# A two-layer diffusion step on eight cores: a generated order per engine, tiles without halo columns, the residual in DRAM, and softmax sums in column tiles

## The chip, the cores and the metric

The kernel runs on all eight cores of one Trainium2 chip, two dies of four cores. Each core computes the same program on its own share of the batch. The metric is the device time of the slowest core, in microseconds (us). Some executions fall in a slow state, in which one die is granted a lower TensorE clock (one of experiment 1: 0.84 against 0.93, and 3288.53 us); verdicts use fast runs alone. A *ratio* below is the mean time of one kernel's fast runs over that of the kernel before in the same rounds on the same chip, with a 95% interval, so it is not quite the ratio of the medians quoted beside it, which are over all executions, slow ones too.

## The reference, cut to what matters

Two layers. Layer 0 mixes tokens with a gated short convolution, layer 1 with grouped-query attention (eight query heads, two key/value heads of 128). After each comes a feed-forward block with a width-3 depthwise convolution. RMS norms stand before and after each sub-layer.

```python
def short_conv_mixer(u, w_in, conv_k, w_out):
    b_gate, c_gate, xp = jnp.split(u @ w_in, 3, axis=-1)
    return (b_gate * dwconv3(c_gate * xp, conv_k)) @ w_out
def conv_ffn(u, w_up, conv_k, w_down):
    h = dwconv3(u @ w_up, conv_k)          # (B, L, 2*D_FF)
    g, up = jnp.split(h, 2, axis=-1)
    return (jax.nn.silu(g) * up) @ w_down
def gated_residual(h, y, g, gate):
    return h + gate * rms_norm(y, g)
# per layer (shortened):
#   u = rms_norm(h, g) * (1 + scale) + shift;  h = gated_residual(h, mixer(u), ...)
#   u = rms_norm(h, g) * (1 + scale) + shift;  h = gated_residual(h, conv_ffn(u), ...)
```

A core holds 3072 tokens of 1024 features: one sample of 2048 tokens, cut into the units S0 and S1 of 1024, and four prompts of 256, the unit PU. S0 and S1 are neighbours in the convolutions. A sample's queries attend to 2560 keys (512 cached), a prompt's to its own 256.

## The kernel before

It is tuned by hand. The text order of the program is the order on each engine, and Python generators are woven by fixed ratios. The second half of an output projection's residual update is *deferred*: it is put, two feature blocks at a time, between pieces of the next stage. Both of its operations run on VectorE (DVE).

```python
                def pair(p):
                    for m in (2 * p, 2 * p + 1):
                        ... P.op("dve", lambda e, m=m: e.scalar_tensor_tensor(   # y = y * gate * rstd
                        ... P.op("dve", lambda e, m=m: e.tensor_tensor(          # h = h + y
                if ct == 0:
                    for p in range(4):
                        pair(p)
                else:
                    for p in range(4):
                        deferred_tail.append((p, lambda p=p: pair(p)))
```

The softmax sums are a 128-row matmul with a matrix of ones for every key chunk, as long as the value matmul beside it.

```python
                def pv(item, first, last):
                    ... e.matmul(bank(ob, NQ), vb[:, vch, j * 128:(j + 1) * 128], pt[pi][:, 0:NQ], ...
                    ... e.matmul(bank(db, NQ), ones, pt[pi][:, 0:NQ], start=first, stop=last)
                ...
                    if ki == min(1, len(keys) - 1) and pending_fin:
                        pending_fin.pop(0)()
```

The whole residual `h` stays in SBUF, the core's working memory. The convolution's inputs are computed with one or two extra halo columns per tile, the neighbours that the width-3 convolution needs (2688 small matmuls), in two sets of three banks of PSUM, the memory in which matmul results land.

Of the kernel before, what the change touches and what calls it, by code (L numbers as in the profile page):

```python
# [11 lines left out]
D = 1024  # L12
# [9 lines left out]
UW = 1032  # L22
# [11 lines left out]

class Prog:
    def __init__(self, nc, es):
        self.nc = nc
        self.engs = {"pe": nc.tensor, "act": nc.scalar, "dve": nc.vector, "pool": nc.gpsimd, "sp": nc.sync}
        self.sems = {}
        self.cnt = {}  # L40
        for e in self.engs:
            self.sems[e] = es.enter_context(nc.semaphore("s_" + e))
            self.cnt[e] = 0
        self.dsem = {}
        self.dcnt = {}
        self.dnext = {"pool": 0, "sp": 0}
        self.ND = 12
        for q in ("pool", "sp"):
            for i in range(self.ND):
                k = "d_%s%d" % (q, i)  # L50
                self.sems[k] = es.enter_context(nc.semaphore(k))
                self.cnt[k] = 0
        self.waited = {}
        self.lastw = {}
        self.readers = {}
        self.out_events = []

    def _need(self, reads, writes):
        need = {}

        def add(ev):
            if ev is None:
                return
            k, v = ev
            if need.get(k, 0) < v:
                need[k] = v
        for r in reads:
            add(self.lastw.get(r))
            if isinstance(r, tuple) and r[0] == "ps":
                for ev in self.readers.get(r, ()):  # L70
                    add(ev)
        for w in writes:
            add(self.lastw.get(w))
            for ev in self.readers.get(w, ()):
                add(ev)
        return need

    def _emit_waits(self, e, need):
        eng = self.engs[e]
        for k, v in need.items():  # L80
            if e == "pe" and k == "pe":
                continue
            if self.waited.get((e, k), 0) < v:
                eng.wait_ge(self.sems[k], v)
                self.waited[(e, k)] = v

    def _record(self, ev, reads, writes):
        for r in reads:
            self.readers.setdefault(r, []).append(ev)
        for w in writes:  # L90
            self.lastw[w] = ev
            self.readers[w] = []

    def op(self, e, fn, reads=(), writes=()):
        need = self._need(reads, writes)
        self._emit_waits(e, need)
        ins = fn(self.engs[e])
        self.cnt[e] += 1
        ins.then_inc(self.sems[e], 1)
        ev = (e, self.cnt[e])  # L100
        self.waited[(e, e)] = max(self.waited.get((e, e), 0), 0)
        self._record(ev, reads, writes)
        return ev

    def dma(self, q, out, in_, reads=(), writes=(), is_output=False):
        i = self.dnext[q]
        self.dnext[q] = (i + 1) % self.ND
        k = "d_%s%d" % (q, i)
        need = self._need(reads, writes)
        if self.cnt[k] > 0:  # L110
            need[k] = max(need.get(k, 0), self.cnt[k])
        self._emit_waits(q, need)
        self.engs[q].dma_start(out=out, in_=in_).then_inc(self.sems[k], 16)
        self.cnt[k] += 16
        ev = (k, self.cnt[k])
        self._record(ev, reads, writes)
        if is_output:
            self.out_events.append(ev)
        return ev

    def barrier(self, engs=("pe", "act", "dve")):
        for e in engs:
            need = {p: self.cnt[p] for p in engs if self.cnt[p] > 0}
            self._emit_waits(e, need)

    def finish(self):
        need = {}
        for k, v in self.out_events:
            need[k] = max(need.get(k, 0), v)
        self._emit_waits("sp", need)  # L130

def run(gen):
    for _ in gen:
        pass

def weave(main, side, per):
    main = iter(main)
    side = iter(side)
    credit = 0.0
    m_alive = True  # L140
    s_alive = True
    while m_alive:
        try:
            next(main)
        except StopIteration:
            m_alive = False
            break
        credit += 1.0
        while s_alive and credit >= per:
            credit -= per  # L150
            try:
                next(side)
            except StopIteration:
                s_alive = False
    if s_alive:
        for _ in side:
            pass

def build_program():
# [21 lines left out]
    rrot = din("rrot", [128, 128])  # L181
    h_out = dout("h_out", [128, KC, TT])
    k_out = dout("k_out", [128, 2, TP])
    v_out = dout("v_out", [TP, 256])

    with ExitStack() as es:
        P = Prog(nc, es)

        def sb(name, cols, dt):
            return es.enter_context(nc.sbuf_tensor(name, [128, cols], dt))  # L190

        h_t = sb("h", KC * TT, F32)
        ru_t = sb("ru", KC * UW, BF16)
        ry_t = sb("ry", KC * 516, F32)
        ra_t = sb("ra", NCF * 1024, BF16)
        wsl_t = [sb("wsl%d" % i, 3072, BF16) for i in range(3)]
        SQ = [sb("sq%d" % i, 512, BF16) for i in range(4)]
        FB = [sb("fb%d" % i, 512, F32) for i in range(4)]
        par_t = sb("par", P_N, F32)
        ones_t = sb("ones", 128, BF16)  # L200
        rrot_t = sb("rrotsb", 128, F32)
        silu_t = sb("silu", 16, BF16)
        modT_t = sb("modT", 2 * 96, F32)
        coef_t = sb("coef", 2 * 64, F32)
        hsave_t = sb("hsave", KC, F32)
        dummy_t = sb("dmy_scr", 2, F32)
        ps_t = es.enter_context(nc.psum_tensor("ps", [128, 4096], F32))

        h = h_t[:].rearrange("p (k t) -> p k t", k=KC)
        u = ru_t[:].rearrange("p (k t) -> p k t", k=KC)  # L210
        ybuf = ry_t[:].rearrange("p (k t) -> p k t", k=KC)
        evq = [ry_t[:, 516 * i:516 * i + 512] for i in range(8)]
        EVQK = [("RY", i) for i in range(8)]
        ev = [ry_t[:, i * 1032:(i + 1) * 1032] for i in range(4)]
        EVK = [[("RY", 2 * i), ("RY", 2 * i + 1)] for i in range(4)]
        pt = [ry_t[:, 516 * (4 + i):516 * (4 + i) + 256].bitcast(BF16) for i in range(4)]
        PTK = [("RY", 4 + i) for i in range(4)]
        a3 = ra_t[:].rearrange("p (c t) -> p c t", c=NCF)
        ps = ps_t[:]
        par = par_t[:]  # L220
        ones = ones_t[:]

        def bank(b, n=512, off=0):
            return ps[:, b * 512 + off: b * 512 + off + n]

        def switch_view():
            pass

        P.dma("sp", par, params, writes=["par"])
        def load_x(ui, after=()):  # L230
            for kc in range(KC):
                P.dma("sp", h[:, kc, ui * 1024:(ui + 1) * 1024], x_in[:, kc, ui * 1024:(ui + 1) * 1024],
                      reads=list(after), writes=[("h", kc, 2 * ui), ("h", kc, 2 * ui + 1)])
        load_x(0)
        P.dma("sp", rrot_t[:], rrot, writes=["rrot"])
        P.op("dve", lambda e: e.memset(ones, 1.0), writes=["ones"])
        P.op("act", lambda e: e.activation(out=silu_t[:], in_=par[:, P_CVEC:P_CVEC + 16], func=AF.Silu),
             reads=["par"], writes=["silu"])
        eps_ap = par[:, P_EPS:P_EPS + 1]

        wstate = {"i": 0}

        def load_w(src, ncols):
            i = wstate["i"]
            wstate["i"] = (i + 1) % 3
            P.dma("pool", wsl_t[i][:, 0:ncols], src, writes=[("w", i)])
            return i

        def wv3(i, inner, nk=KC):
            return wsl_t[i][:, 0:nk * inner].rearrange("p (k n) -> p k n", n=inner)  # L250
# [4 lines left out]
        def mod_gen(l, parts):  # L255
            mv, cf = mvs[l], cfs[l]
            g = lambda which: par[:, P_GAIN + l * 32 + which * 8: P_GAIN + l * 32 + which * 8 + 8]
            for part in parts:
                for bi in range(4):
                    blk = part * 4 + bi  # L260
                    si = load_w(modw[l, blk], KC * 256)
                    w3 = wv3(si, 256)
                    for j in range(2):
                        ch = blk * 2 + j

                        def f(e, w3=w3, j=j, ch=ch):
                            for kc in range(KC):
                                ins = e.matmul(bank(6, 2, ch * 2), w3[:, kc, j * 128:(j + 1) * 128],
                                               silu_t[:, kc * 2:kc * 2 + 2], start=(kc == 0), stop=(kc == KC - 1))
                            return ins  # L270
                        P.op("pe", f, reads=[("w", si), "silu"], writes=[("ps", 6)])
# [49 lines left out]
        def vcols(flat, U, shift):  # L321
            if U.sample:
                return flat[:, 1 + shift:1025 + shift]
# [643 lines left out]
```

## Time and profile before

The time before is 3163.78 us, the median of three runs (3155.91 to 3164.3).

| of the profiled core | before |
|---|---|
| TensorE (PE) busy, and idle | 2731.7, 435.8 us |
| of the busy time, lost to the clock at half speed or at 0.81 | 75 us |
| PE busy less that loss, the *floor* | 2657 us |
| DVE, ACT, POOL busy | 1763, 1484, 229 us |

The loss is worked out from the trace: busy time in each stretch of lower clock, times one minus that clock.

### The profile page before, as it was taken

To read this page: it belongs to the slowest core of one execution; us is meant where nothing else is said; L and a number is where in the kernel's file an instruction comes from. 1 tells how busy PE (TensorE), PEld (TensorE's weight loads), DVE (VectorE), ACT (ScalarE), POOL (GpSimd) and SP (SyncE) were. 2 spreads that over 40 slices of the span, in tenths; PEclk is the share of its full clock that TensorE was granted. 3 is DMA by queue.
4 is the path that set the end of the run, shared out by engine and by line. 5 is a ranking of instruction groups with operands and counts; after the bars stand their busy time and mean duration, and the time that the engine had idled before them with its cause. 6 is when DMAs were issued, how large, how long until landed. Compare 5 with 4: busy or idle time off the path is not lost.

```text
span 3167.5 us, 44493 instructions; the slowest of 8 cores (3146.7 to 3167.5 us)
## 1 busy us (share of the span) xinstructions
PE 2731.7 (86%) x15052; PEld 1245.2 (39%) x15052; DVE 1763.1 (56%) x2113; ACT 1484.0 (47%) x2387; POOL 229.0 (7%) x435
## 2 busy tenths in 40 slices
PE   1889897899899989996799979997779998998997
PEld 0434343344344444442234324443234444443443
DVE  2354555785577477545434363433368647846762
ACT  2142424444344433343588648875834434443432
POOL 0010101000001001000000100001000000000000
PEclk9999999999999999998999999999989999999999
DMA  8655454336555745652100310015234474365347
GB/s 190 114 90 99 71 97 67 64 68 107 93 107 107 127 87 94 108 106 54 30 1 1 54 27 1 1 16 96 35 59 73 84 132 98 67 119 127 67 82 151
DMA packets 72203, 251.16 MB, mean 79 GB/s; under 512 B 7984, under 2 KB 9520, under 8 KB 71984
## 3 DMA queue, kind: packets, MB, share of 16 engines
q0 software_dynamic: 62192, 217.61, 40.7%
q1 hardware_dynamic: 9792, 30.72, 2.9%
q8 instruction: 127, 2.08, 0.3%
q14 instruction: 92, 0.75, 0.1%
HBM read 451.19 MB, written 14.68 MB: 147 GB/s over the span
## 4 chain that ended last, share of the span: by engine, by line
PE 64%; DVE 14%; ACT 8%; DMA 7%; issue 6%; SPq 0%; DVEq 0%; ACTq 0%; POOLq 0%; POOL 0%
PE ps L478 29%; PE ps L421 16%; PE ps L743 5%; PE ps L745 4%; PE ps L753 4%; DVE ry L566 3%; DVE ry L569 3%; PE ps L608 2%; DVE ry L448 2%; DVE h L451 2%; DMA wsl<-wup 2%; DMA wsl<-wo 1%; DMA h<-x_in 1%; ACT ry L561 1%; DVE fb L384 1%
## 5 line engine op out<-in xcount | busy, mean ns | idle before, releaser
L478 PE MATMUL ps<-ru,wsl 128*128 128x512 bf16 (+2 forms) x8064 | 1298.0, 313 | 109.8 <-DVE ry L569 75.6
L478 PEld LDWEIGHTS ps<-ru,wsl 128*128 128x128 bf16 x8064 | 620.2, 98 | 787.5 <-issue 176.8
L421 PE MATMUL ps<-ra,wsl 128*128 128x512 bf16 x2880 | 666.2, 385 | 33.4 <-DMA wsl<-wo 12.6
L566 DVE SCALAR_TENSOR_TENSOR ry<-ps,par,ry 128x1024 f32<-128x1024 f32 x264 | 338.5, 1282 | 193.2 <-ACT ry L558 119.4
L421 PEld LDWEIGHTS ps<-ra,wsl 128*128 128x128 bf16 x2880 | 280.7, 99 | 379.0 <-issue 67.9
L755 ACT ACTIVATE ry<-ps 128x512 bf16<-128x512 f32 x672 | 387.7, 596 | 83.0 <-PE ps L753 41.1
L569 DVE SCALAR_TENSOR_TENSOR ry<-ps,par,ry 128x1024 f32<-128x1024 f32 x264 | 338.8, 1283 | 28.3 <-DVE ry L566 0.9
L384 DVE SCALAR_TENSOR_TENSOR fb<-h,coef,fb 128x512 f32<-128x512 f32 (+2 forms) x296 | 173.6, 587 | 233.7 <-ACT fb L336 233.5
L743 PE MATMUL ps<-ry,ra 128*128 128x512 bf16 x672 | 257.2, 383 | 42.3 <-ACT ry L755 27.0
L448 DVE SCALAR_TENSOR_TENSOR ry<-ry,coef,fb 128x512 f32<-128x512 f32 x192 | 143.2, 746 | 236.9 <-ACT fb L336 236.9
L770 DVE RECIPROCAL fb<-ps 128x512 f32<-128x512 f32 x32 | 107.4, 3358 | 275.8 <-PE ps L745 247.7
L745 PE MATMUL ps<-ry,ones 128*128 128x512 bf16 x672 | 257.3, 383 | 0.0
L435 ACT ACTIVATE ry<-ps 128x512 f32<-128x512 f32 x192 | 113.6, 591 | 299.8 <-PE ps L421 249.9
L753 PE MATMUL ps<-ra 128*128 128x512 bf16 x672 | 245.0, 382 | 7.5 <-DVE ry L640 4.7
L558 ACT ACTIVATE ry<-ps,par 128x513 f32<-128x513 f32 x176 | 121.2, 689 | 204.1 <-PE ps L478 202.8
L556 ACT ACTIVATE ry<-ps,par 128x511 f32<-128x511 f32 x176 | 120.9, 687 | 204.7 <-PE ps L478 126.2
L561 ACT ACTIVATE ry<-ps,par 128x1024 f32<-128x1024 f32 x88 | 98.1, 1114 | 244.2 <-PE ps L478 205.1
L361 ACT ACTIVATE sq<-h 128x512 bf16<-128x512 f32 (+2 forms) x296 | 136.8, 496 | 158.4 <-PE ps L366 126.3
L366 PE MATMUL ps<-sq,ones 128*128 128x512 bf16 (+2 forms) x320 | 93.0, 320 | 118.4 <-ACT sq L361 114.4
L573 DVE TENSOR_TENSOR ra<-ry 128x1024 bf16<-128x1024 f32 x132 | 161.7, 1225 | 14.5 <-DVE ry L569 0.9
L387 DVE TENSOR_SCALAR ru<-fb,modT 128x512 bf16<-128x512 f32 (+2 forms) x320 | 127.1, 397 | 35.5 <-DVE fb L384 1.4
L451 DVE TENSOR_TENSOR h<-h,ry 128x512 f32<-128x512 f32 x192 | 132.9, 692 | 20.3 <-DVE ry L448 0.5
(69 smaller groups left out, 1717.6 us busy)
## 6 DMA issues: line engine op xcount, KB each, us to landing
wsl<-wup POOLq DMA_DIRECT2D x132, 512.0 KB, 5.3
wsl<-wdn POOLq DMA_DIRECT2D x96, 704.0 KB, 7.4
wsl<-modw POOLq DMA_DIRECT2D x48, 512.0 KB, 7.0
wsl<-win POOLq DMA_DIRECT2D x24, 768.0 KB, 7.6
h<-x_in SPq DMA_DIRECT2D x24, 512.0 KB, 17.5
wsl<-wout POOLq DMA_DIRECT2D x48, 256.0 KB, 4.2
wsl<-wo POOLq DMA_DIRECT2D x48, 256.0 KB, 4.4
h_out<-h SPq DMA_DIRECT2D x24, 512.0 KB, 2.8
```

The costliest lines, as they stand in the source:

```text
L384: P.op("dve", lambda e, kc=kc, t=t: e.scalar_tensor_tensor(out=t[:, 0:n], in0=hsrc(kc), scalar=cf[:, ai, kc, U.v:U.v + 1], in1=FB[0][:, 0: ...
L421: ins = e.matmul(bank(b), w3[:, k, :], rhs_fn(k, ct), start=(k == 0), stop=(k == nk - 1))
L448: P.op("dve", lambda e, m=m: e.scalar_tensor_tensor(out=ybuf[:, m, 0:512], in0=ybuf[:, m, 0:512], scalar=cf[:, gi, m, U.v:U.v + 1], in1=FB ...
L451: P.op("dve", lambda e, m=m: e.tensor_tensor(out=h[:, m, hc0:hc0 + 512], in0=h[:, m, hc0:hc0 + 512], in1=ybuf[:, m, 0:512], op=ALU.add), r ...
L478: ins = e.matmul(ps[:, T0 * 512 + c0:T0 * 512 + c0 + n], lhs_fn(kc), u[:, kc, c0:c0 + n], start=(kc == 0), stop=(kc == KC - 1))
L566: P.op("dve", lambda e, rc=rc, zf=zf, s=s, c=c: e.scalar_tensor_tensor(out=rc, in0=vcols(zf, U, -1), scalar=fck(0, s, c), in1=rc, op0=ALU. ...
L569: P.op("dve", lambda e, rc=rc, zf=zf, s=s, c=c: e.scalar_tensor_tensor(out=rc, in0=vcols(zf, U, 1), scalar=fck(2, s, c), in1=rc, op0=ALU.m ...
L573: P.op("dve", lambda e, c=c: e.tensor_tensor(out=a3[:, c, :], in0=ev[eg][:, 0:1024], in1=ev[eg + 1][:, 0:1024], op=ALU.mult), reads=EVK[eg ...
L743: P.op("pe", lambda e: e.matmul(bank(ob, NQ), vb[:, vch, j * 128:(j + 1) * 128], pt[pi][:, 0:NQ], start=first, stop=last), reads=[PTK[pi], ...
L745: P.op("pe", lambda e: e.matmul(bank(db, NQ), ones, pt[pi][:, 0:NQ], start=first, stop=last), reads=[PTK[pi], "ones"], writes=[("ps", db)])
L753: P.op("pe", lambda e: e.matmul(v3(bank(sbank, NQ)), kt[:, j, k0:k0 + 128], q_ap, start=True, stop=True), reads=["KT", "QK"] + qkeys + KA, ...
L755: P.op("act", lambda e: e.activation(out=pt[pi][:, 0:NQ], in_=bank(sbank, NQ), func=AF.Exp, scale=att_scale), reads=[("ps", sbank)], write ...
```

## The change

The intent is to keep TensorE fed and to give it less to do. Each operation is recorded with its dependences, a priority and an assumed duration. A list scheduler then picks, for each engine, the most urgent operation that is ready, and emits that as a fixed order. Tiles are 1024 tokens; only S0 computes one boundary column, and S1 takes its own from a saved column. PSUM gives three sets of two banks. One unit's `h` is written to DRAM and read back between stages, which frees SBUF for a weight ring of 23 slots. Half of the squares, nearly all residual additions and the gate product go to GpSimd (POOL). The softmax sums become 32-row matmuls into four column tiles, whose reciprocal is spread over 128 rows by four small fp32 matmuls. The core of the diff (some 1600 lines long):

```diff
+    def schedule(self):
+        ...
+                i = heapq.heappop(r)[1]          # most urgent of the ready operations of engine e
+            o.t0 = max(t, o.ready)
+            free[e] = o.t0 + o.busy              # assumed duration
...
-                        P.op("dve", lambda e, m=m: e.tensor_tensor(
-                            out=h[:, m, hc0:hc0 + 512], in0=h[:, m, hc0:hc0 + 512], in1=ybuf[:, m, 0:512], op=ALU.add),
...
-                        deferred_tail.append((p, lambda p=p: pair(p)))
+                    if final and ct == 1 and m % 2 == 0:
+                        P.dve(fa, 512, yk + hk(U, m, ct), hk(U, m, ct))
+                    else:
+                        P.pool(fa, 512, yk + hk(U, m, ct), hk(U, m, ct))
+                    ...
+                    elif ct == 1:
+                        store_h(U, m)
...
-                    P.op("pe", lambda e: e.matmul(bank(db, NQ), ones, pt[pi][:, 0:NQ], start=first, stop=last),
+                                for g in range(4):
+                                    ins = e.matmul(ps[32 * g:32 * g + 32, 6 * 512:6 * 512 + 256], ones[:, 0:32],
+                                                   pt[:, g * 256:(g + 1) * 256], start=(ki == 0), stop=(ki == nk - 1))
...
-                pending_fin.append(fin)
+                b = [0, 2][bkc["a"]]
+                bkc["a"] = 1 - bkc["a"]
+                def fb(e, b=b, rc=rc):
+                    for g in range(4):
+                        ins = e.matmul(bank(b + g // 2, 256, (g % 2) * 256), sel_t[:, g * 128:(g + 1) * 128], rc, start=True, stop=True)
```

## The prediction

> **What bounds the kernel now.** I began with the page's busy times and the chain that ended last:
>
> ```profile
> span 3167.5 us, 44493 instructions; the slowest of 8 cores (3146.7 to 3167.5 us)
> PE 2731.7 (86%) x15052; PEld 1245.2 (39%) x15052; DVE 1763.1 (56%) x2113; ACT 1484.0 (47%) x2387; POOL 229.0 (7%) x435
> PE 64%; DVE 14%; ACT 8%; DMA 7%; issue 6%; SPq 0%; DVEq 0%; ACTq 0%; POOLq 0%; POOL 0%
> ```
>
> TensorE is the bound, but a third of the chain runs through other things, and POOL is nearly free. To see where, I cut the span at the first matmul of each stage. The columns are: stretch, length, then busy time of PE, weight loads, DVE, ACT, POOL, granted clock, DMA share, GB/s.
>
> ```profile
> 0.00:83.90 83.90, 14.26 (x152) 6.38 (x153) 22.63 (x57) 17.04 (x33) 6.16 (x15) 1.00 0.83 179
> 190.50:250.70 60.20, 43.59 (x169) 17.61 (x170) 32.37 (x66) 33.81 (x66) 8.65 (x16) 0.87 0.50 80
> 600.00:720.00 120.00, 118.17 (x751) 57.56 (x750) 97.80 (x79) 58.40 (x79) 8.47 (x16) 1.00 0.39 68
> 1115.70:1312.60 196.90, 173.76 (x1249) 85.66 (x1249) 148.30 (x133) 71.31 (x68) 17.94 (x34) 0.97 0.53 94
> 740.70:831.60 90.90, 85.14 (x392) 38.02 (x393) 36.02 (x68) 35.95 (x67) 8.98 (x17) 1.00 0.70 124
> 1451.20:1545.60 94.40, 71.71 (x285) 30.61 (x285) 47.75 (x74) 39.16 (x68) 5.81 (x11) 0.98 0.20 31
> 1545.60:1779.30 233.70, 218.81 (x977) 92.19 (x978) 83.38 (x70) 195.55 (x340) 0.00 (x0) 0.99 0.02 5
> ```
>
> They are, in order: the start, one conv output projection, a steady piece of an FFN up-projection, a whole one (prompt unit), an FFN down-projection, one attention input (q/k/v), one attention sweep. The steady piece is a full TensorE; everything else has holes, the short conv output most, and there the clock falls as well. The groups, shapes apart (count, busy us, mean ns, idle before):
>
> ```profile
> L478 PE MATMUL ps<-ru,wsl 128*128 128x512 bf16 x5376 | 1253.6, 387 | 109.8 <-DVE ry L569 75.6 <-DMA wsl<-wup 8.6 <-DVE hsave L340 4.6
> L478 PE MATMUL ps<-ru,wsl 128*128 128x2 bf16 x1792 | 76.6, 164 | 0.0
> L745 PE MATMUL ps<-ry,ones 128*128 128x512 bf16 x672 | 257.3, 383 | 0.0
> L755 ACT ACTIVATE ry<-ps 128x512 bf16<-128x512 f32 x672 | 387.7, 596 | 83.0 <-PE ps L753 41.1 <-DVE ra L643 15.9 <-PE ps L745 2.6
> L770 DVE RECIPROCAL fb<-ps 128x512 f32<-128x512 f32 x32 | 107.4, 3358 | 275.8 <-PE ps L745 247.7 <-PE ps L366 17.6 <-PE ps L753 10.5
> ```
>
> L478 waits for DVE L569, the last reader of a PSUM set: the two three-bank sets are too few. L745 are the 672 softmax-denominator matmuls.
>
> In the steady piece, matmuls start 0.2155 us apart (timeline), whatever their 0.38 us "duration". One pass there takes 7.66 us for 32 such matmuls and 16 halo ones, so a halo costs (7.66 − 6.90)/16 = 0.048 us.
>
> **What the Trainium skill says.** (1) "TensorE: Matmul & The Clock Gate", Single matmul latency and Back-to-back issue gap: a warm matmul starts every N/2.4 + 2.5 ns; Part 1: after an idle window the clock halves. The trace agrees: 215.5 ns, and 0.87 granted in the holed stage. (2) The same page, Part 3: three column tiles of 32 run 2.38 times faster than one after another. The kernel before has none. (3) "GPSIMD Engine Reference", section 3.1: a two-input fp32 elementwise of 2048 columns takes 4497 ns there, twice VectorE. Before has no elementwise on POOL. (4) "SBUF — State Buffer", SBUF: two separate sides: GpSimd and a VectorE operation with two SBUF inputs exclude each other. No run shows it yet.
>
> **The change, part by part.** First TensorE's floor (matmuls only, warm), counts from the built programs.
>
> Before: 11,308 matmuls of 512 columns (pairs of 256 counted as one) x 0.2155 = 2437; 2688 halos x 0.048 = 129; 768 modulation matmuls at 0.035 (0.56 per 16) = 27; 40 fp32 rotations at 1.165 (46.6/40) = 47. Sum 2640. So 3167 − 2640 = 527 us are holes and slow clock.
>
> After: 10,620 x 0.2155 = 2289; 832 halos (only the first sample unit now computes one boundary column) = 40; modulation 27; rotations 47; 168 sets of eight 32-row, 256-column denominator matmuls; 96 fp32 broadcasts of the reciprocal at 0.58 (half a rotation) = 56. A set one after another is 8 x 0.109 = 0.87 us; at the skill's 2.38 it is 0.37; I take 0.40 (estimate), 67 us. Sum 2526, that is 114 below: halos −89, denominators 145 − 67 − 56 = −22, one normalization fewer −3.
>
> Now the holes, by stage; each sum is before (windows) → floor after + holes left.
>
> *Start* 84 → 68. Weight ring of 23 slots instead of three buffers, so modulation and conv weights stream ahead, and the first x arrives in halves. The weights and x still take their 15 MB (84 us x 179 GB/s), so I take off only 16.
>
> *Conv input* 302 → 1152 x 0.2155 + 128 halos + 16 modulation blocks (9) = 263, + 8 = 271.
>
> *Conv output* 172 → 480 x 0.2155 = 103, + 20 = 124. The holes are squares, evictions and tail updates in a hand-woven order; now half of the squares and nearly all residual adds go to POOL, each output weight is loaded once instead of twice, and the ready instruction goes first. ACT would need some 30 us of 35, DVE 32, POOL 8 squares and 16 adds at about 1.2 = 29: full, but under TensorE.
>
> *FFN up* 1127 → 4224 x 0.2155 + 704 halos + 24 modulation blocks = 958, + 40 = 998. Three two-bank PSUM sets: a set fills in 3.45 us and drains through ACT 1.11, DVE 1.28, DVE 1.28 and hand-overs, about 4.2; three sets give 10.3 us for this 7.7, two gave 7.7 for 8.1. DVE falls from 6.4 to 5.1 us per pass (product to POOL, about 2.3 of 6.9).
>
> *FFN down* 554 → 497 + 57 = 554: no gain. The 704 KB weights land 7.4 us after issue (DMA view), three buffers hold 3 x 4.75 us, and issue sits on POOL. The order of the built program puts eight residual adds (8 x 1.2 = 10 us, more if DVE holds the port) in a row between the weight loads at the middle of each stage. Loads then come late by what the weave's holes lost before.
>
> *Attention* 928 → 760. Inputs of both sample units 216 → 148: one stage for k, v and q instead of a separate k/v pass of the first unit (the normalization repeated), 20 chains x 3.1 us (nine matmuls and a rotation) + 7 for v = 69, + 5. The sweeps 467 → 404: per key chunk and two heads, TensorE 4 x 0.2155 + 0.20 = 1.06, ACT one exp over 1024 columns about 1.03 (0.60 for 512 before); 160 x 1.1 = 176 per unit, and 8 ends with the broadcast 2.3 and the single PV set's copy-out 1 = 26. Three output projections 140 → 111; prompt input and sweep 105 → 97.
>
> Sum 68 + 271 + 124 + 998 + 554 + 760 = 2775, 12% below 3167. Of the 392 us, 114 is fewer matmul cycles and 278 is holes. The residual's trips through DRAM (144 transfers of 512 KB, 75 MB, against 12 MB saved on duplicated weights) lie beside long up-projections whose DMA share is 0.39 to 0.53; I count nothing.
>
> **Rivals.**
> *POOL becomes the wait.* It goes from 0.23 ms to some 0.95 ms: 132 products x 2.3 + 364 smaller operations x 1.2 + DMA issue 0.2. For: it also issues every weight load, in order, and shares a port with DVE; twelve stage ends, each with a run of eight adds beside eight two-input DVE operations, could cost 8 us each, so about 2870. Against: 30% mean load.
> *Column tiles don't overlap.* Then a set is 0.87, a step 1.3, and the sweeps are as long as before: + 75, about 2850. If they overlap fully, ACT takes over at 1.03 per step: 10 less.
> *The schedule is static.* Its order was made for assumed durations; engines run strictly in it, so one late DMA (x took 17.5 us to land when queues were full) stalls all. For: both h buffers wait for a store and a reload. Against: these have 80 us or more, except at the attention input, where the second unit's reload starts only after the prompt unit's last store. Worth 20 to 60 us.
> *A denser TensorE gets a lower clock.* 0.81 shows for 15 us on one die before; the FFN piece at 98% busy held 1.00. I give it little.
> *Better than this:* with holes halved again, 2680.
>
> **Range and chances.** Holes left are 249 us of my sum (2775 − 2526), against 527 before. Holes of 160 give 2690; the POOL and column-tile rivals together give 2900. So 2685 to 2900. To be within 2% of before, nearly all holes would have to stay though their causes are removed: 3%. Slower: 1%.
>
> **What would show it right or wrong.** Right: PE busy near 2600; steady up-projection passes of 6.9 us (7.3 to 7.7 in the first unit) with almost no DVE wait before L537; halo busy near 40 us; sweeps near 202 us; POOL busy near 950. Wrong: exp groups with PE waits and denominator groups of 0.1 us per matmul (tiles serial); TensorE waits on weight DMAs behind POOL adds, longer than a few us; products on POOL well over 2.3 us; normalization waiting for reloaded h; granted clock under 0.96 in dense stages.

## More of the kernel before

The prediction shows the page's lines. Two things more are needed for comparison: how long the update's two operations took while both stood on DVE (count, busy us, mean ns, idle before), and how PE waited for DVE (line waiting, releaser, total us, times, longest):

```profile
L448 DVE SCALAR_TENSOR_TENSOR ry<-ry,coef,fb 128x512 f32<-128x512 f32 x192 | 143.2, 746 | 236.9 <-ACT fb L336 236.9
L451 DVE TENSOR_TENSOR h<-h,ry 128x512 f32<-128x512 f32 x192 | 132.9, 692 | 20.3 <-DVE ry L448 0.5
PE ps L478 <- DVE ry L569: 75.6, 67, 4.8
```

"Faster by so many us" is always the difference of two ratios, times 3165.

## The result, and the profile after

The changed kernel takes 3079.09 us (3077.11 to 3082.86, four runs) against 3163.07 (four runs): ratio 0.9737 [0.9721, 0.9753]. It is faster by 2.6%, not by 12%, and lies outside the predicted range. The page of the changed kernel, profiled run:

```profile
span 3077.8 us, 38746 instructions; the slowest of 8 cores (3052.2 to 3077.8 us)
PE 2633.7 (86%) x13935; PEld 1156.6 (38%) x13935; DVE 1544.0 (50%) x1631; ACT 1292.6 (42%) x1692; POOL 1031.6 (34%) x891
PEclk9998999999899999998999989998599999998998
PE 67%; DMA 10%; issue 8%; DVE 7%; ACT 4%; POOL 3%; SPq 2%; DVEq 0%; ACTq 0%; POOLq 0%
```

PE's busy time fell as it should, but its share stayed at 86%, and in one slice the granted clock is only five tenths. Worked out as before, PE's floor is now 2531 us (2657 before; predicted 2640 and 2526). Idle time is 444 us (436 before) and the clock's loss 103 (75 before). So the whole gain is the fewer matmul cycles, 126 us, and holes and clock took 36 of them back. By stage, in us:

| stage | before | predicted | after | last version below |
|---|---|---|---|---|
| start | 84 | 68 | 80 | 80 |
| conv in + conv out | 474 | 395 | 436 | 417 |
| FFN up | 1127 | 998 | 1025 | 1009 |
| FFN down | 554 | 554 | 605 | 540 |
| attention | 928 | 760 | 933 | 798 |
| sum | 3167 | 2775 | 3078 | 2845 |

One boundary moved: the new order starts S0's value projection inside the FFN down before it, so that the row FFN down holds 14 us of attention work after (8.0 and 6.3) and 7 in the last version, and none before.

Which waits are the holes? The view of PE's waits (line waiting, releaser, total us, times, longest):

```profile
PE ps L490 <- DMA wr<-wdn: 51.8, 11, 9.3
PE ps L438 <- POOL sqa L436: 48.8, 17, 15.0
PE ps L763 <- ACT ev L97: 47.5, 54, 1.4
PE ps L537 <- DVE ev L562: 34.5, 4, 9.7
PE ps L705 <- DVE yb L726: 26.6, 16, 16.5
PE ps L771 <- DVE ev L787: 19.4, 8, 11.7
```

L490 is the down and output projection, L438 the sum of squares of a norm, L537 the up-projection and the conv input, L705 a q/k projection, L763, L771 the attention's scores and values. The kernel before waited often and briefly (L478 on DVE 67 times, longest 4.8 us); this one waits seldom and long. After such a gap the clock is halved: 366 us of the span at half clock on this core, 215 on the profiled core before.

The update's two operations, now on two engines:

```profile
L508 DVE SCALAR_TENSOR_TENSOR yb<-yb,coef,rs 128x512 f32<-128x512 f32 x120 | 170.2, 1484 | 265.0 <-ACT rs L97 265.0
L512 POOL TENSOR_TENSOR h<-h,yb 128x512 f32<-128x512 f32 x116 | 185.4, 1629 | 52.7 <-DVE yb L508 52.7
L627 POOL TENSOR_TENSOR ra<-ev 128x1024 bf16<-128x1024 f32 x132 | 310.4, 2351 | 419.1 <-DVE ev L562 289.0
```

L508 is the same operation as L448 before, and takes twice as long (1484 against 746 ns) when an addition on POOL runs beside it. Where that bites is seen at the start of an up-projection (timeline: start, length, operation, idle before):

```profile
1074.54 11.44 DVE L508 SCALAR_TENSOR_TENSOR yb<-yb,coef,rs 128x512 f32<-128x512 f32 x8 [37.04 <-ACT rs L97]
1075.44 12.89 POOL L512 TENSOR_TENSOR h<-h,yb 128x512 f32<-128x512 f32 x8 [3.38 <-DVE yb L508]
1085.90 4.83 DVE L562 SCALAR_TENSOR_TENSOR ev<-ps,par,ev 128x1020 f32<-128x1020 f32 x4
1089.69 0.58 PE L537 MATMUL ps<-u,wr 128*128 128x512 bf16 x1 [8.13 <-DVE ev L562]
```

All eight updates go ahead of the operation that empties PSUM, the three sets fill, and PE stops for 8.13 us. The same run of eight on POOL, in the middle of a down-projection, holds up the weight loads that POOL issues:

```profile
2757.99 12.89 POOL L512 TENSOR_TENSOR h<-h,ev 128x512 f32<-128x512 f32 x8 [4.02 <-DVE ev L508]
2770.83 1.63 POOL L110 DMA_DIRECT2D wr<-wdn  x3
```

Three loads of 704 KB are issued at once after the run; until then they were issued one per 4.96 us. The last pattern is the end of an attention job (lines between these are left out):

```profile
1617.82 0.60 PE L771 MATMUL ps<-ev,ra 128*128 128x512 bf16 x2
1620.66 1.75 DVE L788 RECIPROCAL rc<-ps 128x256 f32<-128x256 f32 x1
1622.55 1.97 PE L794 MATMUL ps<-rc,selsb 128*128 128x256 f32 x8
1624.62 1.22 DVE L799 TENSOR_TENSOR ra<-ev,ps 128x1024 bf16<-128x1024 f32 x1 [2.22 <-PE ps L794]
1625.99 0.59 PE L763 MATMUL ps<-ra 128*128 128x512 bf16 x2 [1.04 <-DVE ra L799]
1628.35 1.06 PE L771 MATMUL ps<-ev,ra 128*128 128x512 bf16 x2
```

The broadcast of the reciprocal (L794) takes one of only two score sets (pairs of PSUM banks that hold an attention job's scores). The next job's scores for that set must wait for reciprocal, broadcast and product, and the value matmuls, which come in key order, wait behind them. A job takes 28.1 us; its 20 key steps at the 1.085 us of the steady stretch and one broadcast would be 23.7.

### The profile page after: what moved, and what is told of

Same layout as the page of the kernel before. It is cut to its first block, busy times and chain, and to the rows that moved or that the text cites. A ratio compares the mean times of both kernels' runs of the same rounds, so it can differ in the third digit from the quotient of the medians.

```text
span 3077.8 us, 38746 instructions; the slowest of 8 cores (3052.2 to 3077.8 us)
## 1 busy us (share of the span) xinstructions
PE 2633.7 (86%) x13935; PEld 1156.6 (38%) x13935; DVE 1544.0 (50%) x1631; ACT 1292.6 (42%) x1692; POOL 1031.6 (34%) x891
## 4 chain that ended last, share of the span: by engine, by line
PE 67%; DMA 10%; issue 8%; DVE 7%; ACT 4%; POOL 3%; SPq 2%; DVEq 0%; ACTq 0%; POOLq 0%
PE ps L537 32%; PE ps L490 16%; PE ps L763 5%; PE ps L771 4%; DMA wr<-wdn 3%; PE ps L705 2%; POOL h L512 2%; DMA h<-h_mem 2%; ACT ev L97 2%; DVE yb L508 2%; PE ps L794 2%; SPq L110 2%; DMA h<-x_in 2%; PE ps L780 2%; DVE ev L562 1%
## 5 line engine op out<-in xcount | busy, mean ns | idle before, releaser
L537 PE MATMUL ps<-u,wr 128*128 128x512 bf16 x5376 | 1214.1, 385 | 62.5 <-DVE ev L562 34.5
L537 PEld LDWEIGHTS ps<-u,wr 128*128 128x128 bf16 x5376 | 522.9, 99 | 691.7 <-issue 105.4
L562 DVE SCALAR_TENSOR_TENSOR ev<-ps,par,ev 128x1023 f32<-128x1023 f32 (+1 forms) x528 | 675.3, 1281 | 117.3 <-ACT ev L97 71.7
L490 PE MATMUL ps<-ra,wr 128*128 128x512 bf16 x2752 | 645.7, 389 | 65.8 <-DMA wr<-wdn 51.8
L97 ACT ACTIVATE ev<-ps 128x1024 bf16<-128x1024 f32 (+2 forms) x432 | 398.7, 952 | 523.6 <-PE ps L763 212.4
L97 ACT ACTIVATE ev<-ps,par 128x1024 f32<-128x1024 f32 x264 | 294.0, 1114 | 455.0 <-PE ps L537 450.2
L627 POOL TENSOR_TENSOR ra<-ev 128x1024 bf16<-128x1024 f32 x132 | 310.4, 2351 | 419.1 <-DVE ev L562 289.0
L490 PEld LDWEIGHTS ps<-ra,wr 128*128 128x128 bf16 x2752 | 272.6, 100 | 408.9 <-issue 104.6
L508 DVE SCALAR_TENSOR_TENSOR yb<-yb,coef,rs 128x512 f32<-128x512 f32 x120 | 170.2, 1484 | 265.0 <-ACT rs L97 265.0
L771 PE MATMUL ps<-ev,ra 128*128 128x512 bf16 x672 | 209.5, 398 | 21.8 <-DVE ev L787 19.4
L787 DVE COPY ev<-ps 128x1024 f32<-128x1024 f32 x24 | 29.4, 1224 | 349.5 <-PE ps L771 349.5
L512 POOL TENSOR_TENSOR h<-h,yb 128x512 f32<-128x512 f32 x116 | 185.4, 1629 | 52.7 <-DVE yb L508 52.7
L508 DVE SCALAR_TENSOR_TENSOR ev<-ev,coef,rs 128x512 f32<-128x512 f32 x72 | 97.0, 1417 | 166.0 <-ACT rs L97 166.0
L763 PE MATMUL ps<-ra 128*128 128x512 bf16 x352 | 110.2, 396 | 44.8 <-ACT ev L97 25.3
```

The costliest lines, as they stand in the source:

```text
L97: return self._add("act", lambda e: e.activation(out=out, in_=in_, func=func, **kw), reads, writes, busy, busy + 0.12, table=self.TABLES.g ...
L490: ins = e.matmul(bank(b), w3[:, k, :], rhs_fn(k, ct), start=(k == 0), stop=(k == nk - 1))
L508: P.dve(lambda e, y=y, m=m, rs=rs: e.scalar_tensor_tensor(out=y, in0=y, scalar=cf[:, gi, m, U.v:U.v + 1], in1=rs, op0=ALU.mult, op1=ALU.mu ...
L512: fa = lambda e, y=y, hh=hh: e.tensor_tensor(out=hh, in0=hh, in1=y, op=ALU.add)
L537: ins = e.matmul(bank(b + ct), lhs_fn(kc), ub.ap[:, kc, ct * 512:ct * 512 + 512], start=(kc == 0), stop=(kc == KC - 1))
L562: P.dve(lambda e, ro=ro, zi=zi, w=w: e.scalar_tensor_tensor(out=ro, in0=zi, scalar=w, in1=ro, op0=ALU.mult, op1=ALU.add), 1024, rd + wr, wr)
```

## The experiments

There were twelve runs, all edits of the kernel after. The first four share one chip, the next four a second and the last four a third, each with its own runs of the kernel before (medians 3165.04, 3162.35, 3164.88). The kernel after itself had the ratio 0.9737 at first and 0.9782 on the third chip (experiment 9), so a gain of experiments 1 to 4, taken from 0.9737, may be off by some 14 us; the stages in the traces tell where it lies.

### 1. All additions on DVE

```diff
-                    if final and ct == 1 and m % 2 == 0:
+                    if True:
                         P.dve(fa, 512, yk + hk(U, m, ct), hk(U, m, ct))
```

> All residual adds go from POOL to DVE. Theory 'shared port': in the changed kernel the tail's DVE updates (two SBUF inputs) take 1.42 to 1.48 us beside POOL adds of 1.63 us, against 0.75 us in the kernel before; without POOL adds they return to about 0.75 us, the TensorE waits for down-projection weights (52 us in eleven waits) fall under 10 us because POOL issues them at once, and the time falls by 45 to 70 us. The waits at the start of the up-projections stay at 8 to 10 us, because DVE then does sixteen operations of 0.72 = 11.5 us where it did eight of 1.43 = 11.4. Rival 'static order': the holes come from an order made for wrong durations; then the time moves by under 15 us and the holes turn up elsewhere.

Measured: 3011.18 us, ratio 0.9506 [0.9488, 0.9523], that is 73 us faster than the kernel after ((0.9737 − 0.9506) x 3165). The two operations in its trace:

```profile
L508 DVE SCALAR_TENSOR_TENSOR yb<-yb,coef,rs 128x512 f32<-128x512 f32 x120 | 84.6, 748 | 218.9 <-ACT rs L97 218.9
L512 DVE TENSOR_TENSOR h<-h,yb 128x512 f32<-128x512 f32 x120 | 77.3, 686 | 0.0
PE ps L490 <- DMA wr<-wdn: 4.6, 8, 1.4
```

DVE took on 188 additions and its busy time *fell*, from 1544.0 to 1512.4 us: the additions cost 129 us (188 x 686 ns), the updates beside them gave back 137 (192 x 0.71), and other operations the rest. PE's wait for down-projection weights fell from 51.8 to 4.6 us. The six down-projections went from 605 to 535 us, the second conv input from 118.5 to 110.2.

### 2. Weight loads ahead of POOL's arithmetic

```diff
-            P.dma("pool", ap, src, cols * 2 * 128, writes=keys)
+            at(P.prio - 40.0, lambda: P.dma("pool", ap, src, cols * 2 * 128, writes=keys))
```

> Weight loads get precedence over all POOL work in the scheduler (priority 40 us earlier); the adds stay on POOL. Theory 'late issue': the weights wait behind a run of eight adds (12.9 us), so TensorE's 52 us of waits for down weights fall under 15 us and the time falls by 40 to 55 us, while the DVE updates stay at 1.45 us. If instead it is the port contention or the DMA itself that makes the weights late, the waits stay over 35 us and the time moves by under 15 us.

Measured: 3031.24 us, 0.9577 [0.9557, 0.9596], 51 us faster:

```profile
PE ps L490 <- DMA wr<-wdn: 23.6, 15, 3.9
```

The wait fell, though not under the 15 us expected, and the six down-projections went from 605 to 562 us. This and experiment 1 treat the same stretch from two sides, so their gains do not add: with the additions off POOL (and experiments 3 and 4 in), the scheduler plans the same time, 2784 us, with and without this edit.

### 3. The eight updates after an output phase at a later priority

```diff
+                late = ct == 1 and not final and (l == 0 and not (gi == 3 and U is PU) or l == 1 and gi == 3)
+                p_end = P.prio
                 for m in range(KC):
+                    P.prio = p_end + (4.0 * (m + 1) if late else 0.0)
```

> The second half's residual updates get later priorities, one per 4 us, so that the next stage's PSUM evictions stand before them on DVE. Theory 'burst before evictions': TensorE's waits for DVE at the start of the up-projections (8 to 10 us in each of five) fall under 3 us, and the time falls by 35 to 55 us; port contention and late weights stay (updates 1.4 us, 52 us of weight waits). Rival 'static order' or a normalization that waits longer for its reloaded h: under 15 us, or slower.

Measured: 3072.57 us, 0.9706 [0.9692, 0.9721]: 10 us, within the uncertainty named above, and the expectation missed. In the trace, PE's idle time in the six up-projections went from 65 us only to 56. In three of them it shrank (8.1 to 4.9, 8.7 to 4.1, 8.1 to 1.0 us), in the others (S0 in both layers, S1 in the first) it stayed or grew; the condition `late` leaves out the output phase before S0's in the second layer. The updates are still as long beside POOL. What the edit does without that is seen in experiment 10.

### 4. The end of an attention job four key steps later

```diff
+                    if pend_fin and ki == min(4, len(keys) - 1):
+                        pend_fin.pop()()
...
-                b = [0, 2][bkc["a"]]
-                P.pe(fb, 4 * 0.43, rck + [("sel",)], pk(b, b + 1))      # and the product after it
+                pend_fin.append(fin)        # fin: the same lines, taking its set when it is called
```

> The end of each attention job (broadcast of the reciprocal and multiplication) is emitted four key steps into the next job, so the score set it takes is no longer blocked through the reciprocal. Theory 'job end blocks a score set': a job of 20 steps falls from 28.1 us to about 24 (20 x 1.085 + 1.97 for the broadcast), the two sweeps from 225 and 254 us to about 192 and 215, the prompt sweep from 90 us to about 60; in all 80 to 110 us faster. Rival 'ACT is the bound in the sweeps' (exp 1.0 us per step): the sweeps stay above 215 and the time falls by under 30 us.

Measured: 2993.79 us, 0.9457 [0.9441, 0.9472], 89 us faster: the largest single part. The windows of the three sweeps, first of the kernel after, then of this one (stretch, length, busy time of PE, weight loads, DVE, ACT, POOL, granted clock, DMA share, GB/s):

```profile
1510.00:1734.50 224.50, 199.19 (x1341) 73.33 (x1340) 31.75 (x26) 157.89 (x162) 5.25 (x5) 0.98 0.01 2
1764.60:2018.70 254.10, 211.06 (x1374) 77.55 (x1373) 60.84 (x64) 169.00 (x182) 28.66 (x24) 0.93 0.14 40
2142.90:2232.70 89.80, 57.16 (x190) 23.91 (x186) 29.84 (x23) 17.40 (x18) 0.00 (x0) 0.60 0.00 0
```

```profile
1513.00:1717.00 204.00, 193.25 (x1348) 75.84 (x1346) 31.59 (x26) 157.74 (x164) 5.29 (x5) 1.00 0.01 3
1746.00:1978.00 232.00, 203.20 (x1379) 78.38 (x1377) 60.21 (x63) 168.35 (x184) 28.23 (x24) 0.96 0.15 44
2102.00:2149.00 47.00, 33.99 (x185) 17.33 (x182) 29.61 (x23) 16.79 (x18) 0.00 (x0) 0.96 0.00 1
```

The work is the same; the stretches shrink by 20, 22 and 43 us. The sample sweeps stayed above the 192 and 215 us expected, the prompt sweep went below its 60. The prompt sweep shows the clock at work: eight short jobs of two key steps each, a gap in every one, the clock at 0.60, so that even PE's *busy* time was 57 instead of 34 us.

### 5. The three edits together

Experiments 1, 3 and 4 in one kernel.

> The three single edits together: all residual additions on DVE, the finish of an attention job deferred by four steps, and the eight updates after an output phase given a later priority. If the causes are separate, the gains add: measured from the after kernel, 70 + 88 + 10 = 168 us, so about 2910 us. If they overlap (the adds and the late priority act on the same stretch), 2930 to 2950. If a third limit takes over (late h and weights), above 2950.

Measured: 2899.96 us, but only one of six executions counted as fast, so there is no ratio. On this chip one die spent some 320 us of the span at a clock of 0.81, the other some 100; the kernel before ran there as on the other chips (3162.35). It was run again (experiment 10).

### 6. The scheduler's durations set to the measured ones, the rest of the kernel after untouched

```diff
-        busy = n / 1200.0 + 0.10 + ap
+        busy = n / 1200.0 + 0.16 + ap
-        rate = 0.165e6 if q == "pool" else 0.30e6
+        rate = 0.165e6 if q == "pool" else 0.18e6
-                        P.pool(fa, 512, yk + hk(U, m, ct), hk(U, m, ct))
+                        P.pool(fa, 690, yk + hk(U, m, ct), hk(U, m, ct))
 # likewise the update on DVE (512 -> 1229 cycles) and the broadcast (0.43 -> 0.49)
```

> Nothing but the scheduler's own table of durations is changed, to what the trace of the after kernel shows (ACT 0.06 us longer, the contended update 1.45 us, the addition on GpSimd 1.64 us, h transfers slower, the reciprocal's broadcast 1.96 us). Rival theory: the loss comes from an order made for wrong durations; then this kernel gains 60 to 150 us (2930 to 3020). My theory: the loss is in the structure (two score sets, shared port), which no order mends; then it stays within 30 us of the after kernel (3050 to 3090). The scheduler's own figure for it is 3071 us against 2906 for the uncalibrated one, so I expect about 3060.

Measured: 3105.33 us, 0.9817 [0.9801, 0.9832], no faster than the kernel after (0.9737, and 0.9782 on the third chip). The chip had its low clock here too (226 to 254 us at 0.81 on one die, 46 us lost on the profiled core). Apart from that, nothing was won: PE's floor is 2529 us and its idle time 417 us, where the kernel after has 444. So some 27 us of the holes, as far as one core of each tells, came from an order made for wrong durations. The plan itself is instructive: the scheduler had assumed 2906 us; with the measured durations it plans 3071, close to what the chip had shown. Told the true durations, the same scheduler found no order without the gaps.

### 7. Experiment 5 with the corrected durations

> The three edits together and the scheduler's table corrected for ACT, the broadcast and the h transfers (nothing contended is left to correct). If wrong durations matter once the structure is mended, 20 to 50 us faster than the run of the three edits alone; if not, within 10 us of it.

Measured: 2934.29 us, again without a ratio; its one fast run, 2922.61, is slower than the one fast run of experiment 5, 2903.4. With one fast run each this is no verdict, but no help from better durations shows once the structure was mended either.

### 8. The four column tiles made one (a wrong result on purpose)

On top of experiment 4, with the reciprocal and broadcast reading those 32 rows:

```diff
-                                    ins = e.matmul(ps[32 * g:32 * g + 32, 6 * 512:6 * 512 + 256], ones[:, 0:32],
+                                    ins = e.matmul(ps[0:32, 6 * 512:6 * 512 + 256], ones[:, 0:32],
```

> Gives a wrong result on purpose. On top of the deferred finish, all four denominator matmuls of a step go to the same 32 columns of the array instead of four different ones; same count, same shapes, same order. If the four column tiles do run beside each other, a set of eight goes from 0.34 us to about 0.87 us and the kernel loses up to 168 x 0.53 = 89 us against the deferred finish alone (2994), so 3060 to 3085; if their overlap is worth nothing on the path, it stays at 2994.

Measured: wrong (relative error 0.065), 3145.07 us. The low clock came on this chip as well, so I read the sweeps alone, which ran at full clock in the stretch shown. A set of eight and the matmul after it, first in experiment 4, then here:

```profile
1606.44 0.40 PE L781 MATMUL ps<-ev,ones 128*32 128x256 bf16 x8
1606.78 0.60 PE L764 MATMUL ps<-ra 128*128 128x512 bf16 x2
```

```profile
1620.38 1.05 PE L781 MATMUL ps<-ev,ones 128*32 128x256 bf16 x8
1621.36 0.60 PE L764 MATMUL ps<-ra 128*128 128x512 bf16 x2
```

From one start to the next is 0.34 us with four tiles and 0.98 with one: the tiles run beside each other. 168 x 0.64 = 108 us, and the three sweeps grew by 50, 46 and 15, together 111. My expected 89 took 0.109 us per matmul; they take 0.98/8 = 0.122. The rest of the difference to experiment 4 lies in other stages, whose matmuls ran at the lower clock: the profiled core lost 63 us to 0.81, and none in experiment 4.

### 9. The control, and two norms later

> The changed kernel once more, unedited, as the control on this chip: about 3079 us as before. In the last batch (another chip) one die spent some 300 us of each denser kernel at a clock of 0.81, which the kernel before did not; if the changed kernel shows that here too it is the chip and not the edits.

Measured: 3094.41 us, 0.9782 [0.9763, 0.9801]. On this third chip the kernel after shows 0.81 for 83 to 104 us on one die and 15 to 30 on the other, where it had none in its first profile. So that clock comes without my edits too. But on this one chip it grows with the denser kernels: the longest on a core is 104 us here, 149 with the two norms later, 208 in experiment 10 and 236 in experiment 11. Experiments 9 to 11 are compared with this 0.9782.

```diff
-        at(p0, lambda: norm(S1, 1, 0, 0, UE))
+        at(p0 + 60.0, lambda: norm(S1, 1, 0, 0, UE))
-        at(p1 + 40.0, lambda: norm(PU, 1, 0, 0, UQ))
+        at(p1 + 80.0, lambda: norm(PU, 1, 0, 0, UQ))
```

> On the changed kernel only the priorities of two input norms are moved later (second sample unit: 60 us into the attention inputs instead of at their start; prompt unit: 80 us into the second sweep instead of 40). My theory: each norm is a burst of some 21 us on DVE, during which TensorE, in order, waits for the vector work that frees its PSUM banks (L705 behind L726 26.6 us in the attention inputs). Then the 38.8 us idle of the attention inputs falls to about 15 and the second sweep loses some 5 us: 20 to 35 us less in all. Rival: the wait is the latency of the chain norm, rotation, product through six banks, whatever else DVE does; then within 8 us of the control.

Measured: 3069.0 us, 0.9692 [0.9669, 0.9716]: 28 us faster ((0.9782 − 0.9692) x 3165). The sum came as expected, its parts did not. In the attention inputs idle time fell only from 40.3 to 31.6 us, and the longest wait of L705 from 16.5 to 4.3:

```profile
PE ps L705 <- DVE yb L726: 13.5, 14, 4.3
```

The second sweep shrank from 255.5 to 235.6 us. In the kernel after, PE had waited 11.7 us there for one job's copy out of PSUM (L787), which stood behind the prompt's norm on DVE; now it waits 0.4. So the burst theory holds. In the inputs 31.6 us stay idle; that these are the chain of latencies, as the rival said, is not shown.

### 10. The three edits together, again

> The three edits together once more, since only one of six executions counted as fast in the last batch: on an undisturbed chip 2860 to 2900 us, 168 us or more below the control of this batch; if the low clock of one die comes back, it belongs to the denser kernel and not to that one chip, and the time is again about 2900.

Measured: 2881.23 us, 0.9091 [0.9068, 0.9113]: 219 us below the control. The single gains of experiments 1, 3 and 4 add up to 172 (73 + 10 + 89). The 47 us between are hardly more than three times the 14 us of uncertainty named above, so the sum alone doesn't show that the edits help each other; the traces do. PE's idle time in the up-projections is 29 us, against 65 in the kernel after, 56 with the later priority alone and 67 with the additions on DVE alone: the later priority is worth more when the updates have half the length. The low clock came back (86 to 208 us at 0.81 on one die, at most 15 on the other), so it is not peculiar to the chip of experiment 5.

### 11. With both norms, six steps and 6 us

Experiment 10 with experiment 9's norms, the finish deferred by six steps instead of four, the updates 6 us apart instead of 4.

> The three edits, with the finish deferred by six steps instead of four and the later updates at steps of 6 us instead of 4, and the two later norms. If the bursts theory holds and adds up, 25 to 45 us below the three edits alone, so 2820 to 2870 us; if the added density only buys a lower granted clock, within 10 us of them.

Measured: 2843.6 us (2838.52 to 2846.71, five runs), 0.8986 [0.8968, 0.9004], correct. This beats both kernels: 10.1% faster than before, 252 us below the control and 33 below experiment 10. Which of its four changes gives how much of the 33 was not tested.

```profile
span 2845.1 us, 38747 instructions; the slowest of 8 cores (2776.9 to 2845.1 us)
PE 2596.3 (91%) x13935; PEld 1155.9 (41%) x13935; DVE 1533.2 (54%) x1819; ACT 1290.4 (45%) x1694; POOL 739.5 (26%) x703
```

PE's floor is 2518 us, idle 249, clock loss 79 (36 at half speed, 43 at 0.81). Half clock is down to 100 to 132 us per core.

## Why the prediction was wrong

**The floor was right.** Predicted 2640 to 2526, read from the traces 2657 to 2531. The halos are gone, the column tiles overlap (0.34 us a set, assumed 0.40; experiment 8 shows what it is worth), a POOL product takes 2.35 us (assumed 2.3), POOL is busy 1032 us (assumed some 950). Three sums of the working slipped without moving this: the conv output's 103 + 20 is 123, holes halved again would give 2650 and not 2680, and the POOL and column-tile rivals together (95 and 75) give 2945 and not 2900; the measured time lies above that too.

**The step that failed is "Holes left are 249 us of my sum".** Holes and clock loss were 547 us, more than the 511 before (436 + 75); the prediction reckoned this older figure at 527. I had worked out that some holes' causes are removed, and they were, but I did not ask what the order would do with what it had been given. Four terms of the sum carry it:

*Attention, 760 against 933.* The term was "8 ends with the broadcast 2.3 and the single PV set's copy-out 1", 3.3 us each. The end cost 6.4 us (28.1 − 20 x 1.085), since the broadcast holds one of two score sets through a chain of three operations; the prompt sweep, eight ends with little between, took 90 us where the prompt's input and sweep together had been given 97. Experiment 4 shows it, 89 us. The kernel before had this end deferred, in lines that I had before me. The inputs, predicted 148, took 173, of which experiment 9 gave back little.

*FFN down, 554 against 605.* The sentence "Loads then come late by what the weave's holes lost before" guessed an even trade. It was a loss of 51 us more, 14 of them the value projection that moved in: experiment 1 brings the stage down to 535, experiment 2 to 562.

*FFN up, 998 against 1025, and the residual adds.* I named the shared port of DVE and POOL but charged the adds about 1.2 us on POOL and nothing on DVE. With nothing beside them they do take 1.26 us, but in the runs of eight they took 1.63 there and doubled the 192 updates on DVE. The run of updates then stood before PSUM's evictions. Experiment 1 is the proof for the port: with the adds off POOL each update is back at 0.75 us. The holes of the up-projections close only when the updates are also put later (experiment 10).

*Conv, 395 against 436.* "I count nothing" for the residual's trips through DRAM was too little, though little of it is the reload itself. PE waits 48.8 us for squares made on POOL (L438 above). Looking at what each square had itself waited for, 24.7 us go to first loads of x, 15.2 to POOL's own queue, and only 8.2 to a reloaded `h`. The longest, 15.0 us in the second conv input, is for the prompts' x, whose buffer had first to be emptied by the store of S0's `h`. In that stage the idle time fell from 27.0 us to 16.6 in experiment 1, and to the same 16.6 in experiment 2 with the adds still on POOL, so it is not the adds' engine alone that decides. What DRAM costs by itself no run here tells apart; the start and the conv stages still stand 34 us above prediction in the last version.

**The rivals.** *POOL becomes the wait* was right in kind and set the right size for its part (95 us predicted, 73 measured in experiment 1), but I gave it as a tail of the range, not as the centre, and it was only one of four. *Column tiles don't overlap* is refuted. *The schedule is static*, for wrong durations, is refuted as the main cause: corrected durations win nothing. The part of it that did show is a buffer that waits for a store (the 15.0 us above). What is static in a harmful way is the priority: work released in a burst goes out in a burst. *A denser TensorE gets a lower clock*: the halved clock after gaps cost 103 us in the kernel after, which I had folded into the holes; 0.81 I had given little, and the last version lost 43 us to it on its slowest core and nothing on the other die.

**What closes the account.** From 3094 (the control) to 2844 are 251 us. In the two profiled executions, 247 us apart, 203 of them are PE's idle time (452 to 249), 30 the clock's loss (109 to 79) and 13 the floor. Of the 69 us left to the predicted 2775, the stage table puts 34 in start and conv, 38 in attention, 11 in FFN up, and −14 in FFN down. That the slowest core of the last version still loses 79 us to the clock is a part of each of these.

## What to carry to other kernels

When a list scheduler replaces a hand-made order, look in the old code for every place that puts work off on purpose, and ask what does this in the new one: a priority by program order releases a burst as soon as it may, and an in-order engine pays for it. Before moving an operation to a "free" engine, ask what it holds while it runs: here 188 additions moved off DVE made DVE busier, and held up the transfers that the other engine issues. And a wait that falls is not a hole that closes: count the floor, the holes and the clock apart, before and after.

## What the Trainium skill lacked or had wrong

- "SBUF — State Buffer", SBUF: two separate sides, calls the pair of ports an exclusive lock held for the whole instruction. The trace agrees in kind and adds the price: the DVE update with two SBUF inputs goes from 0.746 to 1.484 us, and eight pairs take 13.79 us from the first update's start to the last addition's end, 1.72 each. That is less than the two one after another, 0.75 + 1.26 = 2.01 (additions with no DVE operation beside them took 1.25 to 1.26 us in the same trace), so the blocking was not total. "Perfetto Trace Analysis", Optimizing Scalar/DVE Operations, says that moving work between the two engines "might not help"; here it cost 73 us, the weight loads held up behind it included.
- "TensorE: Matmul & The Clock Gate", Part 3, has three column tiles of 32 (2.38 times). No page has a measured figure for four: four column tiles of 32 with 256 moving columns, in sets of eight, gave 0.98/0.34 = 2.9 times.
- The same page, Part 1, has the whole die at 13/16 of the clock soon after a third core becomes dense, for as long as the load lasts, and advises to plan for it. Here all eight cores of the last version had PE at work through a dense program (busy 91% of the span on the slowest and on the fastest core), and four of them spent none of it at 0.81, the other four 103 to 236 us. The kernel before had 15 us on one die. It depended on the chip (the kernel after had none in one profile and 15 to 104 us on another chip) and on the kernel (experiment 9).
- The same page describes matmul bursts that fall back to half clock in every wait for a DMA; no page has a figure for short attention jobs, where the gap is the job's own end: a sweep with a gap in each of its eight jobs had a mean clock of 0.60, and 57 us of PE time for work that takes 34.
